# The output projection of a decoder layer computed by seven block products, with its input passed through DRAM

## The chip, the cores and the metric

The kernel runs on one core of a Trainium2 chip. The metric is the time of one execution on the device in microseconds. The core has a matrix engine (TensorE, PE in the profile; its weight loads are listed apart as PEld), a vector engine (VectorE, DVE), a scalar engine (ScalarE, ACT), a general engine (GpSimd, POOL) and a sync engine (SyncE, SP) whose queue issues all the DMA transfers of this kernel. The engines run side by side and wait for each other by semaphores; each takes its own instructions in order.

## What is computed

One decoder layer for 1024 tokens of width 1024, in float32:

```python
x = x + 0.5 * swiglu(rms_norm(x, ffn1_norm), ffn1_w_gate, ffn1_w_up, ffn1_w_down)
h = rms_norm(x, mix_norm)
...                                     # forgetting attention and stick-breaking attention
merged = (sigmoid(g_fox) * (y_fox @ w_branch_fox)
          + sigmoid(g_sb) * (y_sb @ w_branch_sb))
x = x + merged @ w_out
x = x + 0.5 * swiglu(rms_norm(x, ffn2_norm), ffn2_w_gate, ffn2_w_up, ffn2_w_down)
x = x + sigmoid(rms_norm(x, ple_norm) @ w_ple_gate) * (p @ w_ple_proj)
```

`swiglu(h)` is `(silu(h @ w_gate) * (h @ w_up)) @ w_down` with a hidden width of 2816. `y_fox` and `y_sb` are 1024 x 512, both branch weights 512 x 1024, `w_out` 1024 x 1024. The change is about `merged` and `merged @ w_out`, and about the order of some instructions in both feed-forward passes.

## The kernel before

**Numbers in two parts.** A float32 matrix is split into a high part in a shorter format (a ScalarE copy) and a low part, the rest (a subtraction on VectorE or GpSimd). A product is three matmuls: high by high, high by low, low by high. `split` (L101) does both; `wload` (L108) loads a block of weights into a RAW buffer, and `wsplit` (L120) splits it into WH and WL, its low part in two halves on GpSimd (L129).

**Block products.** The two feed-forward passes use the scheme of Strassen and Winograd: both operands are cut in 2 x 2 blocks, and seven products of sums of blocks take the place of eight. In `ffn` (L213) the up pass computes the seven products for gate and up weights of 256 hidden columns at a time (pairs n of 22 half steps); `evict` (L316) brings each out of PSUM, and `hidden_sums` (L352) makes the four sums of hidden blocks on GpSimd (L356 to L359) that the next product needs and stores them (L360, L361). The seven blocks per pair lie in the DRAM tensor `hidden`. `prep` (L279) splits weights four products ahead of their use, calls `sums` (L269: three sums on GpSimd) for the next pair, and after a pair's fourth block `load`s the weights two pairs on (L242).

The down pass (L426 on) takes the hidden width in three chunks. `wd_block` loads a block of the weights, `wd_sums` makes their sums on VectorE, `load_hid` (L468) fetches one of the seven hidden blocks, `prep_down` splits both into four H buffers (two are in use, two are being filled), and `down` gives the matmuls of one product (four row tiles of 3 x 4 matmuls of 512 columns, L505) and its eviction (L510). The products of one half of the output add up in the same PSUM banks; the result after each is added to the residual in an X buffer. In the last chunk `last_norms` weaves in the next norm.

**Who orders what.** The attention, the branches and the first three quarters of the second half of the output projection are ordered by the compiler's list scheduler (only TensorE's order is given, by `pe`). Both feed-forward passes, with their entries, stand in a manual schedule: each engine's instructions run in the order in which the code emits them. So an instruction that waits holds up everything emitted after it on its engine, and on SP each DMA that waits holds up all later ones.

**Buffers.** `slot(tag, ...)` takes one of a few buffers of 128 partitions (`BUFS`, L30: four H, four T, three WH, WL and PT, two of the others); the first instruction on it waits until the one before is done with. `bank(tag)` does so for the eight PSUM banks; `ps1` takes the four banks of pt and pf in turn, `ps2` the four of sc and av.

**The stretch that changes.** After the attention a loop over eight column tiles m computes `merged`, transposed: per half of the tokens 12 matmuls for the second branch (L1098) and, for m of 4 to 7, 12 for the first (those of m 0 to 3 were done as filling in the attention and lie in A). `gated` loads the gate values, takes the sigmoid on ScalarE and multiplies on VectorE (L1103 to L1105); the two are added (L1236) and split into the buffers `mg`. Then `out_steps` (L1245) goes over halves, four quarters of 256 output columns and four row tiles, with 24 matmuls each (L1253); L1257 adds to the residual, L1260 stores the finished rows, and `out_weights` loads a quarter of `w_out` each time. The norm of the first half is computed along the way (`norm_pre`; `norm_post` turns the result by eight transposes per tile, L190). The last quarter of the second half stands in `second_entry` (L1272), woven with the first steps of the second up pass: `F["load"]`, `F["prep"]`, `F["a"]` (turns and splits of the second half's norm, L366) and `F["plain"]` (products with an operand as it is, L251).

Of the kernel before, what the change touches and what calls it, by code (L numbers as in the profile page):

```python
# [2 lines left out]

# [6 lines left out]
F32 = mybir.dt.float32  # L10
# [25 lines left out]
def tile_hybrid_decoder_layer(  # L36
# [175 lines left out]

    def ffn(N, wg, wu, wd, next_gain, resid, hid, tags, entry, tail):  # L213
# [102 lines left out]
        def evict(n, m, ps):  # L316
# [32 lines left out]
            if m == (4 if n == 1 else 3) and n < nm_ - 1:  # L349
                hidden_sums(n, ("PT", "PT"))  # L350

        def hidden_sums(n, tags):  # L352
            j = n // 2
            g1, g2 = E[n - 1]
            s12, s34 = (slot(t, [P, 2, 512]) for t in tags)
            nc.gpsimd.tensor_add(s12[:, 0, :], g1[:, 1, :], g2[:, 1, :])  # L356
            nc.gpsimd.tensor_sub(s12[:, 1, :], s12[:, 0, :], g1[:, 0, :])
            nc.gpsimd.tensor_sub(s34[:, 0, :], g1[:, 0, :], g1[:, 1, :])
            nc.gpsimd.tensor_sub(s34[:, 1, :], g2[:, 0, :], s12[:, 1, :])  # L359
            nc.sync.dma_start(hid[j, :, 3:5, :], s12[:])  # L360
            nc.sync.dma_start(hid[j, :, 5:7, :], s34[:])  # L361
            del E[n], E[n - 1]
# [62 lines left out]

        PR = ((0, 0, (0, 0)), (1, 1, (0, 0)), (4, 2, (0, 1)), (3, 3, (1, 1)), (6, 4, (0, 1)), (5, 5, (1, 1)), (2, 6, (1, 0)))  # L426
        chunks = [(0, 4), (4, 8), (8, 11)]
        D_ = {}
        OP = {}
        A_ = {}  # L430
        groups = [None, None]
        nxt = []

        def pairs(c):
            j0, j1 = chunks[c]
            return [(j, min(j + 2, j1)) for j in range(j0, j1, 2)]

        def wd_block(c, k, dh, tags):
            out = []
            for (j0, j1), tag in zip(pairs(c), tags):  # L440
                t = slot(tag, [P, 2, 512])[:, 0:j1 - j0, :]
                nc.sync.dma_start(t, wdown[k][:, j0:j1, dh * 512:dh * 512 + 512])
                out.append(t)
            D_[c, k, dh] = out

        def wd_sub(o, a, b):
            for x_, y_, z_ in zip(o, a, b):
                nc.vector.tensor_sub(x_, y_, z_)

        def wd_sums(c, m):  # L450

            if m == 1:
                D_[c, "t1"] = [slot("Y", [P, 2, 512])[:, 0:j1 - j0, :] for j0, j1 in pairs(c)]
                wd_sub(D_[c, "t1"], D_[c, 0, 1], D_[c, 0, 0])
            elif m == 2:
                D_[c, "t2"] = [slot("PT", [P, 2, 512])[:, 0:j1 - j0, :] for j0, j1 in pairs(c)]
                wd_sub(D_[c, "t2"], D_[c, 1, 1], D_[c, "t1"])
            elif m == 3:
                wd_sub(D_[c, 0, 1], D_[c, 1, 1], D_[c, 0, 1])
            else:  # L460
                wd_sub(D_[c, 1, 0], D_[c, 1, 0], D_[c, "t2"])

        def load_hid(c, i):
            raw = A_[c, i] = []
            tags = (("GF", "RN"), ("KH", "KL"), ("Q", "Q"))[(7 * c + i) % 3]
            for (j0, j1), tag in zip(pairs(c), tags):
                t = slot(tag, [P, 2, 512])[:, 0:j1 - j0, :]
                nc.sync.dma_start(t, hid[j0:j1, :, PR[i][0], :].rearrange("j p n -> p j n"))  # L468
                raw.append(t)

        def prep_down(c, i):
            raw = A_.pop((c, i))
            wt = D_[c, *((0, 0), (1, 0), ("t2",), ("t1",), (1, 1), (0, 1), (1, 0))[i]]
            OP[c, i] = slot("H", [P, 2, 4, 512], F32R), slot("H", [P, 2, 4, 512], F32R)
            for o, src in zip(OP[c, i], (raw, wt)):
                k = 0
                for s in src:
                    n = s.shape[1]
                    split(o[:, 0, k:k + n, :], o[:, 1, k:k + n, :], s, nc.scalar, nc.vector)
                    k += n  # L480
            if c + 1 < len(chunks):
                if i == 3:
                    wd_block(c + 1, 0, 0, ("WH", "WH"))
                    wd_block(c + 1, 1, 0, (("RAW", "RAW"), ("WL", "WL"))[(c + 1) % 2])
                elif i == 5:
                    wd_block(c + 1, 0, 1, ("T", "T"))
                    wd_block(c + 1, 1, 1, ("T", "T"))
            if c and i < 2 or i in (3, 4):
                wd_sums(c, (1, 2, None, 3, 4)[i])

        def down(c, i):

            g = 0 if i in (0, 2, 5, 6) else 1
            fresh = i in (0, 1, 3)
            if fresh:
                groups[g] = [bank(t) for t in (("sc", "sc", "sc", "av"), ("pt", "pf", "pt", "pf"))[g]]
            act, wt = OP.pop((c, i))
            nk = chunks[c][1] - chunks[c][0]
            half, d = PR[i][2]

            def matmuls(t):
                n = 0
                for a, b in ((0, 0), (0, 1), (1, 0)):
# [21 lines left out]
        with tc.manual_schedule():  # L525
# [35 lines left out]
            for s, (c, i) in enumerate(steps):  # L561
                if s and s + 2 < len(steps):
                    load_hid(*steps[s + 2])
# [817 lines left out]
```

## Time and profile before

| | us |
|---|---|
| median of 3 runs | 2345.83 |
| lowest and highest | 2343.23, 2346.04 |
| the profiled execution, time on the device | 2339.73 |
| its span, first to last instruction | 2338.0 |

| engine | busy, us | share of the span | instructions |
|---|---|---|---|
| TensorE | 2286.0 | 98% | 12238 |
| weight loads | 1960.9 | 84% | 12238 |
| VectorE | 1456.5 | 62% | 2243 |
| ScalarE | 984.1 | 42% | 1753 |
| GpSimd | 833.8 | 36% | 760 |

A profile page describes one execution. "Busy" is the time in which an engine ran an instruction; neighbouring matmuls overlap, so a matmul's own duration is longer than its pitch, and a pitch is had by dividing a gapless stretch by its matmuls. A row of the timeline gives start, length, engine, line, what is written and read, how often, and in brackets how long the engine had stood and for whom. Rows with SPq are DMA issues: their length is the time of issuing; the transfer itself ends later, at the "us to landing" of the DMA list. The chain of waits follows the work that ended last back through what released it. L numbers are lines of the kernel.

The branch products run from 1428.6 to 1495 us of the span, the output projection until about 1591, the second up pass until 2033.

### The profile page before, as it was taken

Reading aid. Unit: us, or ns where it says so; the run is one execution under the profiler, and the core shown is the slowest. Engines: PE = TensorE matmul, PEld = TensorE weight load, DVE = VectorE, ACT = ScalarE, POOL = GpSimd, SP = SyncE. Lnnn points to the kernel's source line nnn. Section 1 sums busy time; section 2 is a strip of 40 time slices with the busy share of each in tenths; the row PEclk is TensorE's granted clock in tenths of the full one; section 3 lists DMA queues with packets and bytes.
Section 4 is the critical chain, followed back from the end, with each engine's and each line's share of the span. In section 5 each row is a group of like instructions: output and inputs, shape, how many; then the busy total and the mean of one; then the engine's idle time right before and its main releaser. Section 6 shows DMA issues by size and latency. Waiting matters only on the chain.

```text
span 2338.0 us, 32373 instructions
## 1 busy us (share of the span) xinstructions
PE 2286.0 (98%) x12238; PEld 1960.9 (84%) x12238; DVE 1456.5 (62%) x2243; ACT 984.1 (42%) x1753; POOL 833.8 (36%) x760
## 2 busy tenths in 40 slices
PE   7999999999999999999998999999999999999999
PEld 6788888888888999988877877898788888888899
DVE  7754555688763656655685567548755555787773
ACT  6333333343352556544554565335333333343441
POOL 2353535300043556544464444100445453300130
PEclk9999999999999999999999999999999999999999
DMA  4232323483332122221213444432323232664232
GB/s 144 86 126 81 122 82 122 153 324 108 123 117 85 42 75 82 78 73 51 77 55 109 131 137 138 131 127 96 109 98 115 89 123 84 227 249 145 82 125 75
DMA packets 197500, 268.52 MB, mean 115 GB/s; under 512 B 27352, under 2 KB 130776, under 8 KB 197344
## 3 DMA queue, kind: packets, MB, share of 16 engines
q1 hardware_dynamic: 197344, 266.45, 33.8%
q8 instruction: 96, 1.57, 0.3%
q14 instruction: 60, 0.49, 0.1%
HBM read 188.78 MB, written 69.24 MB: 110 GB/s over the span
## 4 chain that ended last, share of the span: by engine, by line
PE 87%; DVE 6%; ACT 3%; issue 2%; DMA 1%; POOL 1%; SPq 0%; DVEq 0%; ACTq 0%; POOLq 0%
PE ps L304 31%; PE ps L505 17%; PE ps L616 11%; PE ps L624 10%; PE ps L1253 4%; PE ps L1098 3%; PE ps L916 3%; PE ps L895 2%; PE ps L844 1%; PE ps L843 1%; DVE RN L819 1%; PE ps L261 1%; PE ps L766 1%; PE ps L190 1%; DVE X L103 1%
## 5 line engine op out<-in xcount | busy, mean ns | idle before, releaser
L505 PE MATMUL ps<-H,H 128*128 128x512 f32 x1848 | 422.5, 390 | 0.0
L505 PEld LDWEIGHTS ps<-H,H 128*128 128x128 f32 x1848 | 347.6, 188 | 72.1
L304 PE MATMUL ps<-H,WL 128*128 128x512 f32 x1008 | 244.2, 394 | 0.8 <-ACT WL L102 0.8
L304 PEld LDWEIGHTS ps<-H,WL 128*128 128x128 f32 x1008 | 189.6, 188 | 44.6 <-ACT WL L102 1.6
L624 PE MATMUL ps<-H,WH 128*128 128x512 f32 x768 | 210.7, 402 | 5.0 <-ACT PT L770 2.2
L129 POOL TENSOR_TENSOR WL<-RAW,WH 128x512 fp32r<-128x512 f32 (+1 forms) x112 | 132.4, 1205 | 154.4 <-ACT WH L123 123.1
L616 PE MATMUL ps<-WH,H 128*128 128x256 f32 (+1 forms) x1152 | 164.4, 285 | 3.6 <-DVE KL L693 1.8
L624 PEld LDWEIGHTS ps<-H,WH 128*128 128x128 f32 x768 | 137.4, 189 | 29.0 <-issue 2.5
L898 DVE TENSOR_TENSOR PT<-ps,PT 128x512 fp32r<-128x512 f32 (+1 forms) x160 | 101.3, 634 | 92.4 <-ACT PT L897 91.0
L616 PEld LDWEIGHTS ps<-WH,H 128*128 128x128 f32 x1152 | 148.1, 189 | 5.7 <-issue 2.0
L304 PE MATMUL ps<-H,Q 128*128 128x512 f32 x600 | 143.7, 390 | 0.0
L510 DVE SCALAR_TENSOR_TENSOR X<-ps,X 128x512 f32<-128x512 f32 x168 | 109.0, 683 | 54.6 <-PE ps L505 54.6
L129 POOL TENSOR_TENSOR WL<-Y,WH 128x528 fp32r<-128x528 f32 (+1 forms) x8 | 11.1, 1419 | 359.3 <-PE ps L505 359.3
L304 PEld LDWEIGHTS ps<-H,Q 128*128 128x128 f32 x600 | 112.6, 188 | 24.2
L897 ACT CAST PT<-ps 128x512 fp32r<-128x512 f32 (+1 forms) x160 | 87.1, 546 | 101.0 <-PE ps L895 91.4
L356 POOL TENSOR_TENSOR PT<-GF,RN 128x512 f32<-128x512 f32 x20 | 33.1, 1657 | 256.3 <-issue 147.3
L304 PE MATMUL ps<-X,WL 128*128 128x512 f32 x504 | 123.5, 394 | 0.0
L916 PE MATMUL ps<-PT,X 128*128 128x256 f32 (+1 forms) x640 | 105.5, 284 | 10.2 <-DVE PT L898 9.9
L916 PEld LDWEIGHTS ps<-PT,X 128*128 128x128 f32 x640 | 93.9, 189 | 23.1 <-DVE PT L898 13.5
L304 PEld LDWEIGHTS ps<-X,WL 128*128 128x128 f32 x504 | 94.9, 188 | 21.7
L624 PE MATMUL ps<-H,WL 128*128 128x512 f32 x384 | 107.9, 402 | 0.0
L123 ACT CAST WH<-RAW 128x1024 fp32r<-128x1024 f32 (+1 forms) x72 | 68.2, 955 | 90.4 <-PE ps L1253 41.4
(374 smaller groups left out, 5035.3 us busy)
## 6 DMA issues: line engine op xcount, KB each, us to landing
hidden<-PT SPq DMA_DIRECT2D x40, 512.0 KB, 3.0
WH<-in_ffn_w_gate_dram SPq DMA_DIRECT2D x38, 512.0 KB, 5.2
hidden<-RN SPq DMA_DIRECT2D x22, 512.0 KB, 2.6
Q<-hidden SPq DMA_DIRECT2D x22, 512.0 KB, 7.1
RAW<-in_w_in_dram SPq DMA_DIRECT2D x22, 512.0 KB, 4.0
KH<-in_ffn_w_up_dram SPq DMA_DIRECT2D x20, 512.0 KB, 5.9
KL<-in_ffn_w_up_dram SPq DMA_DIRECT2D x20, 512.0 KB, 6.5
T<-in_ffn_w_down_dram SPq DMA_DIRECT2D x20, 512.0 KB, 5.0
```

Source lines behind the costliest of these rows:

```text
L123: order("wh", nc.scalar.copy(hi[:], raw[:]))
L129: ins = eng_lo.tensor_sub(lo[part], raw[part], f(hi[part]))
L304: pe(nc.tensor.matmul(ps[:], hl[:, a, k, :], rhs(m, b, k), start=(first and i == 0), stop=(final and i == 11), skip_group_check=True))
L505: pe(nc.tensor.matmul(groups[g][t][:], act[:, a, k, t * P:(t + 1) * P], wt[:, b, k, :], start=(fresh and n == 0), stop=(i in (6, 1, 4) and ...
L510: nc.vector.scalar_tensor_tensor(xs, groups[g][t][:], 0.5, xs, ALU.mult, ALU.add)
L616: pe(nc.tensor.matmul(ps[:, :n], hT[t // 4][a][:, k, (t % 4) * P:(t % 4 + 1) * P], w[k // 4][b][:, k % 4, :n], start=(i == 0), stop=(i == ...
L624: pe(nc.tensor.matmul(ps[:], w[a][:, k, :], hT[half][b][:, k, :], start=(i == 0), stop=(i == 23)))
L897: nc.scalar.copy(pt[:, 0, :width], ps[:, :width])
L898: low = nc.vector.tensor_sub(pt[:, 1, :width], ps[:, :width], f(pt[:, 0, :width]))
L916: pe(nc.tensor.matmul(o, lh, r, start=(kpair == c and i == 0), stop=(kpair == 0 and i == 3)))
L1098: pe(nc.tensor.matmul(ps[:], w[a][:, k, :], yT[g][b][:, k, half * 512:half * 512 + 512], start=(i == 0), stop=(i == 11)))
L1253: pe(nc.tensor.matmul(ps[:, :256], mg[half][k // 2][a][:, k % 2, col:col + P], w[k // 4][b][:, k % 4, :], start=(i == 0), stop=(i == 23)))
```

## The change

1. *Shared code.* The four block sums and their stores become the function `block_sums(out, g1, g2, tags)`. The down pass's helpers become `make_down(wdown, hid, chunks, scale, sum_tags)`; `ffn` uses it with scale 0.5. In `prep` the weights are now split before the activations.
2. *Up passes.* `hidden_sums` is no longer called at the end of `evict` but after the `prep` that follows it in the loop, so that `prep`'s sums and loads are emitted first.
3. *Branches.* The first branch's tiles m = 4 to 7 are computed ahead of all of the second's, into A. The second's are gated, added to A, and not split: each pair of m is two blocks of 512 x 512 halves, stored to the new DRAM tensor `branch_sums` with its four sums, made on GpSimd.
4. *Projection.* `second_entry` loads the seven block sums back and runs the down pass's seven products once over all of the width, with `w_out` as weights and scale 1. The norms of both halves are woven into products 4 to 6, and the second up pass follows.

```diff
+    PR = ((0, 0, (0, 0)), (1, 1, (0, 0)), (4, 2, (0, 1)), (3, 3, (1, 1)), (6, 4, (0, 1)), (5, 5, (1, 1)), (2, 6, (1, 0)))
+
+    def block_sums(out, g1, g2, tags):
+        s12, s34 = (slot(t, [P, 2, 512]) for t in tags)
+        nc.gpsimd.tensor_add(s12[:, 0, :], g1[:, 1, :], g2[:, 1, :])
+        nc.gpsimd.tensor_sub(s12[:, 1, :], s12[:, 0, :], g1[:, 0, :])
+        nc.gpsimd.tensor_sub(s34[:, 0, :], g1[:, 0, :], g1[:, 1, :])
+        nc.gpsimd.tensor_sub(s34[:, 1, :], g2[:, 0, :], s12[:, 1, :])
+        nc.sync.dma_start(out[:, 3:5, :], s12[:])
+        nc.sync.dma_start(out[:, 5:7, :], s34[:])
+
+    def make_down(wdown, hid, chunks, scale, sum_tags):
...
+        def prep(c, i):
+            raw = A_.pop((c, i))
+            wt = D_[c, *((0, 0), (1, 0), ("t2",), ("t1",), (1, 1), (0, 1), (1, 0))[i]]
+            OP[c, i] = slot("H", [P, 2, 4, 512], F32R), slot("H", [P, 2, 4, 512], F32R)
+            for o, src in zip(OP[c, i][::-1], (wt, raw)):
...
+            def evict(t):
+                xs = X[half][:, t, d * 512:d * 512 + 512]
+                if scale == 1.0:
+                    nc.vector.tensor_add(xs, groups[g][t][:], xs)
+                else:
+                    nc.vector.scalar_tensor_tensor(xs, groups[g][t][:], scale, xs, ALU.mult, ALU.add)
...
-            if m == (4 if n == 1 else 3) and n < nm_ - 1:
-                hidden_sums(n, ("PT", "PT"))
...
                 if s + LA < len(seqn):
                     prep(*seqn[s + LA])
+                if n % 2 and m == (4 if n == 1 else 3) and n < nm_ - 1:
+                    hidden_sums(n, ("PT", "PT"))
...
-    mg = [[], []]
-    for m in range(KD):
...
+    od = dp.tile([4, P, 7, 512], F32, name="branch_sums")
+    xm = dp.tile([S, D], F32, name="x_mix")
+    for m in range(4, KD):
+        w = wload([kp(w_branch_fox[0])[:, :, m * P:(m + 1) * P]], 4, P)
+        A.append(slot(("GF", "RN", "Q", "KH")[m - 4], [P, S]))
         for half in range(2):
...
+            ps = ps2()
+            run(branch_steps(ps, 0, m, half, w))
+            gated(A[m][:, half * 512:half * 512 + 512], ps, 0, m, half)
     Xm = [slot("X", [P, 4, D]) for _ in range(2)]
...
+    oproj = make_down(w_out[0].rearrange("(j k p) n -> k p j n", k=2, p=P), od, [(0, 4)], 1.0, ("WH", "PT"))
+    for m in range(KD):
+        w = wload([kp(w_branch_sb[0])[:, :, m * P:(m + 1) * P]], 4, P)
+        g = slot("T", [P, 2, 512])
+        for half in range(2):
             ps = ps1()
...
+            run(branch_steps(ps, 1, m, half, w))
+            gated(g[:, half, :], ps, 1, m, half)
+            nc.vector.tensor_add(g[:, half, :], g[:, half, :], A[m][:, half * 512:half * 512 + 512])
+        if m % 2 == 0:
+            g1 = g
+            nc.sync.dma_start(od[m // 2, :, 0, :], g1[:, 0, :])
+        elif m < KD - 1:
+            nc.sync.dma_start(od[m // 2, :, 1:3, :], g[:])
+            block_sums(od[m // 2], g1, g, ("PT", "PT"))
+        if m == 4:
+            oproj.wd_block(0, 0, 0, ("Y", "Y"))
+    N = []
 
     def second_entry(F):
...
+        oproj.wd_block(0, 1, 0, ("RAW", "RAW"))
+        oproj.wd_block(0, 0, 1, ("T", "T"))
+        oproj.load_hid(0, 0)
+        nc.sync.dma_start(od[3, :, 1:3, :], g[:])
+        oproj.load_hid(0, 1)
+        oproj.wd_block(0, 1, 1, ("WL", "WL"))
+        oproj.prep(0, 0)
+        block_sums(od[3], g1, g, ("PT", "PT"))
+        oproj.load_hid(0, 2)
...
+        for i in range(7):
+            if 0 < i < 5:
+                oproj.load_hid(0, i + 2)
+            if i != 1 and i < 6:
+                oproj.prep(0, i + 1)
+            matmuls, evict = oproj.product(0, i, Xm)
+            if i == 0:
+                for t in range(4):
+                    matmuls(t)
+                oproj.wd_sums(0, 1)
+                oproj.wd_sums(0, 2)
+                oproj.prep(0, 2)
+                for t in range(4):
+                    evict(t)
+                continue
+            if i == 3:
+                N.append(combo_begin(Xm[0], ffn2_norm[0]))
+                N.append(combo_begin(Xm[1], None, N[0]))
+            elif i == 6:
+                F["load"](0)
+            for t in range(4):
+                matmuls(t)
+                evict(t)
+                if i == 4:
+                    finished(0, t)
+                    norm_stat(N[0], t, ("WL", "WL", "WL", "WH")[t])
+                elif i == 5:
+                    norm_mul(N[0], t)
+                elif i == 6:
+                    finished(1, t)
+                    norm_stat(N[1], t, ("PT", "PT", "WH", "KL")[t])
+                    norm_post(N[0], t, ps1)
+                    if t:
+                        norm_mul(N[1], t - 1)
+                    if t == 2:
+                        F["prep"](0, 1)
+        F["load"](1)
         F["a"](0)
...
+        norm_mul(N[1], 3)
         F["prep"](0, 2)
         F["prep"](0, 5)
         F["a"](1)
         F["plain"](0, 0, (0,))
...
         F["prep"](0, 4)
         F["a"](2)
         F["plain"](0, 0, (1,))
```

More of the change, by code (lines that the diff above doesn't have):

```diff
@@ L463, in load_hid @@
[L463 to L503, printed above, removed]
-                    for k in range(nk):
-                        pe(nc.tensor.matmul(groups[g][t][:], act[:, a, k, t * P:(t + 1) * P], wt[:, b, k, :], start=(fresh and n == 0), stop=(i in (6, 1, 4) and n == 3 * nk - 1), skip_group_check=True))
-                        n += 1
-            def evict_down(t):
-                xs = X[half][:, t, d * 512:d * 512 + 512]
-                nc.vector.scalar_tensor_tensor(xs, groups[g][t][:], 0.5, xs, ALU.mult, ALU.add)
-            return matmuls, evict_down
+        down = make_down(wdown, hid, [(0, 4), (4, 8), (8, 11)], 0.5, ("Y", "PT"))
```

205 lines of the change are left out of this document (87 added, 118 removed).

## The prediction

> **What bounds the kernel now.** I read the page first, then a table of busy time for the stretches around the change, then the chain of waits there, then what TensorE waited for in each pass.
>
> ```profile
> PE 2286.0 (98%) x12238; PEld 1960.9 (84%) x12238; DVE 1456.5 (62%) x2243; ACT 984.1 (42%) x1753; POOL 833.8 (36%) x760
> ```
> ```profile
> 1428.60:1495.00 66.40, 66.40 (x291) 54.27 (x290) 40.66 (x59) 31.25 (x53) 14.77 (x18) 1.00 0.57 182
> 1495.00:1587.00 92.00, 92.00 (x780) 92.00 (x780) 43.16 (x76) 26.75 (x36) 4.76 (x12) 1.00 0.37 121
> 1587.00:1611.00 24.00, 23.60 (x130) 20.01 (x129) 18.88 (x32) 17.99 (x36) 1.58 (x4) 1.00 0.47 153
> ```
>
> The first stretch is the branch products, the second the output projection, the third the entry into the second up pass; after the time stand the busy times of PE, PEld, DVE, ACT and POOL. TensorE is never free in the first two and lacks 0.4 us in the third. In the projection the weight loads are busy all the time too: a 256-column matmul is too short to cover its load. So this change is paid in TensorE time, and every wait that it brings into these stretches is added in full.
>
> ```profile
> 1428.61 66.38 PE ps L1098 x288
> 1494.99 46.90 PE ps L1253 x396
> ...
> 1547.51 0.87 PE ps L190 x8
> ```
> ```profile
> 2032.86 183.84 PE ps L505 x811
> ```
>
> These are pieces of the chain of waits. A branch product of 512 columns takes 66.38/288 = 0.2305 us, a projection matmul of 256 columns 46.90/396 = 0.1184, eight transposes 0.87, a down-pass product 183.84/811 = 0.2267.
>
> **Part 1: fewer columns in the projection.** Removed: 2 halves x 4 column quarters x 4 row tiles x 24 = 768 matmuls at 0.1184 = 91.0 us. Added: 7 products x 4 tiles x 12 = 336 of the down pass's form at 0.2267 = 76.2 us. The branch matmuls stay 288 and the transposes of the norm stay 64. Result **-14.8 us**. [...] The trace has 118 and 227 ns with the weight loads in the stream, and I go by it.)
>
> **Part 2: up-pass sums behind the next loads.** The longest waits of TensorE in the first up pass (first fence: in total, times, longest) and one of the second:
>
> ```profile
> PE ps L304 <- ACT Y L324: 2.2, 1, 2.2
> PE ps L304 <- ACT WL L102: 0.6, 1, 0.6
> ```
> ```profile
> PE ps L304 <- ACT Y L324: 1.1, 1, 1.1
> ```
> ```profile
> 86.39 0.34 SPq L345 DMA_DIRECT2D hidden<-RN  x1
> ...
> 94.03 0.32 SPq L361 DMA_DIRECT2D hidden<-PT  x1
> 94.44 1.32 SPq L242 DMA_DIRECT2D WH<-in_ffn_w_gate_dram  x2
> 99.19 0.62 ACT L102 CAST PT<-WH 128x512 fp32r<-128x512 f32 x1 [4.66 <-DMA WH<-in_ffn_w_gate_dram]
> ```
>
> Here is where the first comes from. The sync queue stands from 86.4 to 94.0 us behind the store of GpSimd's sums; the load follows it, ScalarE waits 4.66 us for it, and ScalarE's next copy is what TensorE waits for. With the preparation emitted first the load leaves some 7 us earlier, more than the 2.2 and 1.1 us that are missing: **-3.3 us**, or nothing if another slot holds the load. At later pairs GpSimd takes the two in this order before the change, four hidden sums and then the next weights':
>
> ```profile
> 232.41 1.62 POOL L356 TENSOR_TENSOR PT<-GF,RN 128x512 f32<-128x512 f32 x1 [14.76 <-issue]
> ...
> 237.05 1.74 POOL L359 TENSOR_TENSOR PT<-RN,PT 128x512 f32<-128x512 f32 x1
> 238.75 1.29 POOL L272 TENSOR_TENSOR RAW<-KH 128x512 f32<-128x512 f32 x1
> ```
> ```profile
> 239.22 1.33 SPq L242 DMA_DIRECT2D WH<-in_ffn_w_gate_dram  x2
> ```
>
> Now the weights' three sums (3 x 1.29 = some 4 us) go first, and the hidden sums, their stores and the load at 239 us move back by that. The whole first up pass has no wait but that one above 0.6 us; cost nothing, covered by weights that are prepared four products (11 us) ahead. Without that cover 4 us would come back at up to nine pairs of each pass.
>
> **Part 3: the branch stage.** Each branch product m is 24 matmuls, 5.53 us. What its halves cost VectorE and its weights GpSimd:
>
> ```profile
> 1431.43 0.69 DVE L1105 TENSOR_TENSOR PT<-PT,ps 128x512 f32<-128x512 f32 x1 [0.53 <-PE ps L1098]
> 1432.15 0.69 DVE L1236 TENSOR_TENSOR PT<-PT,Q 128x512 f32<-128x512 f32 x1
> ...
> 1434.71 1.89 POOL L129 TENSOR_TENSOR WL<-RAW,WH 128x256 fp32r<-128x256 f32 x2 [10.66 <-ACT WH L123]
> ```
>
> Product 0 of before ends at 1428.61 + 12 x 0.2305 = 1431.4 and its half is gated and added at 1432.8: 1.5 us. Four block sums take 238.75 - 232.41 = 6.4 us (part 2); with two low parts of weights (1.9 each) GpSimd is busy 10.2 of 11.1 us per pair of m. The sync queue gets 12 more stores here (7.3 MB, and 14 loads to fetch it back), against 16 loads of the output weights that become 8; the last column of the table has 182 and 121 GB/s in these stretches, where 7.3 MB in 66 us add 110. Four PSUM banks let the gating run 11 us behind. Cost nothing, with little room (see the GpSimd rival).
>
> **Part 4: the read-back.** The projection now begins with operands that have been through DRAM, and TensorE has nothing else to do. Let z be the end of the last branch product. The second entry's loads stand on the sync queue behind the stores of the sums of pair 2, and its T loads need these sums' buffers anyway. Product 5 ends at z - 11.1, its half is added at z - 9.6, the sums end at z - 3.2.
>
> ```profile
> 458.17 1.95 SPq L442 DMA_DIRECT2D T<-in_ffn_w_down_dram  x4
> ...
> 461.04 1.41 SPq L468 DMA_DIRECT2D Q<-hidden  x2
> 462.50 4.63 SPq L557 DMA_DIRECT2D X<-in_x_dram  x4
> ```
> ```profile
> hidden<-PT SPq DMA_DIRECT2D x40, 512.0 KB, 3.0
> ```
> ```profile
> RAW<-in_w_out_dram SPq DMA_DIRECT2D x16, 512.0 KB, 3.7
> ```
> ```profile
> Q<-hidden SPq DMA_DIRECT2D x1, 512.0 KB, 9.6
> ```
> ```profile
> X<-in_x_dram SPq DMA_DIRECT2D x1, 512.0 KB, 10.8
> ```
>
> One issue costs 1.95/4 = 0.49 us. The first Q lands at 461.0 + 9.6 = 470.6, the first X, two transfers later, at 462.5 + 10.8 = 473.3: under load they land in order, 1.33 us apart. The last store lands at z - 0.2 (3.0 us), then two RAW, two T, then GF and RN with the first activations: six steps, 7.8 us after z. RN is issued at about z, so 7.8 us is between the 3.7 us of a load alone and the 9.6 of a full queue.
>
> ```profile
> 450.57 1.99 ACT L102 CAST H<-WH 128x1024 fp32r<-128x1024 f32 x2
> 452.41 2.35 DVE L103 TENSOR_TENSOR H<-WH,H 128x1024 fp32r<-128x1024 f32 x2
> ```
>
> A high part takes 1.0 us more, a low part 1.2; the first tile can use GF's half 0.45 us before. TensorE stands **8.4 us** (bounds 4.3 and 10.2, by the two landing times). The second operand's store leaves at z + 1.5 and its read-back lands some 12 us after z, its splits end near z + 15; product 0 ends at z + 19.3. The third (sums of pair 3) lands near z + 21 and is wanted at z + 30. Both covered.
>
> After such a pause TensorE is slow at first:
>
> ```profile
> 7.85 1.97 PE L190 MATMUL ps<-identf,PT 128*128 128x128 f32 x8 [7.85 <-DVE PT L185]
> ...
> 18.49 3.91 PE L261 MATMUL ps<-H,WL 128*128 128x512 f32 x12 [0.33 <-ACT H L102]
> ...
> 23.02 3.02 PE L261 MATMUL ps<-H,WL 128*128 128x512 f32 x12
> ```
>
> The first dense group lost 3.91 - 3.02 = **0.9 us**; bounds 0 and 1.9 (that and the 0.9 of eight transposes). [...]
>
> **Part 5: the entry into the second up pass.** In the last product each tile now brings an eviction, ScalarE's statistics, two turned blocks and a norm multiply, in this order:
>
> ```profile
> 2235.37 1.08 ACT L102 CAST H<-ps 128x512 fp32r<-128x512 f32 x2 [0.88 <-PE ps L190]
> 2235.99 1.29 DVE L103 TENSOR_TENSOR H<-ps,H 128x512 fp32r<-128x512 f32 x2
> 2236.33 1.07 ACT L180 ACTIVATE KH<-X 128x1024 f32<-128x1024 f32 x1
> 2237.20 1.28 DVE L185 SCALAR_TENSOR_TENSOR PT<-X,rs,PT 128x1024 f32<-128x1024 f32 x1
> ```
>
> In the down pass, shown here, the casts run ahead of the statistics. The new code puts the statistics first, so VectorE goes 0.7 evict (as at 1431.43), 1.6 waiting (statistics 1.1, first cast 0.5), 1.2 low parts, 1.2 multiply = 4.7 us per tile against TensorE's 12 x 0.2267 + 0.87 = 3.6. The first tile has no multiply and ends at 6.5 us after that product's start; two full cycles and a weight's low part (0.6) bring the last eviction to 16.6, its end to 17.3, the last low part (1.8 and 1.2 on) to 20.3, and the first plain product, which needs it and the bank of the turn before it (0.8), to 21.1. TensorE ends its tiles and turns at 14.4 and has 1.7 us of turns in between: it stands **5.0 us**. Bounds: 1.7, a stall in the same place of the down pass, and 7.8, if all four tiles run at 4.7 and the last 3 us follow.
>
> ```profile
> 2231.56 1.25 PE L190 MATMUL ps<-identf,PT 128*128 128x128 f32 x8 [1.74 <-DVE H L103]
> ```
>
> The 0.4 us that TensorE lacks in this stretch now goes: **-0.4**.
>
> **Sum.** -14.8 - 3.3 - 0.4 + 8.4 + 0.9 + 5.0 = -4.2 us on the profiled execution's 2339.73, so 2335.5. The runs shown have a median of 2345.83, 6 us above that one; the forecast is 2345.8 - 4.2 = **2341.6**. With all costs low it is -12.5, with all high and no gain in the up passes +4.7.
>
> **The rivals.** (a) *The read-back is hidden*: the chunk changes of the down pass show no wait of TensorE, and SP may get to the loads sooner. Against it: there the operands were stored long before. Sum without 8.4 + 0.9: -13.5, 2332.3. (b) *The entry keeps step*, at the 1.7 us of the down pass: -7.5, 2338.3. Against it, the order of the statistics. (c) *GpSimd becomes the bound of the branch stage*: beside a busy VectorE one of its sums takes 2.16 us.
>
> ```profile
> L357 POOL TENSOR_TENSOR KH<-KH,GF x2: 2155/2160/2165, 459.2 to 2026.4; 128x512 f32<-128x512 f32 x2
> ```
>
> At 4 x 2.2 = 8.8 us it needs 12.6 us per 11.1, is 3 us behind by pair 2, and the read-back comes 2.4 + 3 later: +1.2, 2347.0, with as much again possible where weights wait behind sums. VectorE is busy only 41 of 66 us there, which speaks against it. (d) *Slower by the clock*: after the 8.4 us pause, in product 0, TensorE runs at half rate not for 4 matmuls' worth but for all 48: 48 x 0.2267 = 10.9 in place of 0.9, +5.8, 2351.6. It decides from 23 slow matmuls on (5.1/0.2267, the sum without the 0.9). For it: the transposes stayed at 1.94 until 18 us; against it, the first dense group lost only 0.9.
>
> **How the numbers follow.** Forecast 0.46, (a) 0.17, (b) 0.09, (c) 0.14, (d) 0.14. A measurement of this kernel tells about 0.2% (4.7 us) from no change. The forecast's own range, 2337 to 2346, is cut by that line: 0.20 faster, 0.22 same, 0.04 slower. (a) and (b) are faster; (c) is 0.06 same, 0.08 slower; (d) slower. Faster 0.46, same 0.28, slower 0.26. The range 2332 to 2353 holds all but the ends of (a) and (d).
>
> **What would show it.** 336 matmuls of the down-pass form in about 76 us without the waits; one wait of TensorE for ScalarE's cast of GF or RN of some 8 us just after the last branch product, and slow matmuls behind it; no wait for line 324's copy in either up pass; some 5 us of waits for VectorE before the first plain product. Wrong would be: no wait at the read-back, waits inside the branch stage, or waits at products 1 and 2.

## The result, and the profile after

| | before | after |
|---|---|---|
| median, us | 2344.8 (19 runs) | 2348.67 (19 runs) |
| lowest and highest | 2340.64, 2350.19 | 2343.97, 2352.2 |
| profiled execution | 2339.73, span 2338.0 | 2348.63, span 2346.9 |

The ratio after to before is 1.0016, with a 95% interval of 1.0009 to 1.0024: slower by 0.16%, some 3.8 us (2.1 to 5.6). The forecast was 4.2 us faster. The two profiled executions differ by 8.9 us, more than the medians, because the one of before is among its fastest runs and the one of after is at its median. The 5.1 us between 8.9 and 3.8 have a cause of their own (see the first experiment).

The engines over the span of after:

```profile
PE 2278.3 (97%) x11806; PEld 1937.3 (83%) x11806; DVE 1476.5 (63%) x2227; ACT 982.7 (42%) x1749; POOL 840.2 (36%) x776
```

432 fewer recorded matmuls, and TensorE is no longer at 98%. The table of the stretches of after, cut at its own boundaries (branch products, seven products, entry), columns as in the prediction:

```profile
1431.60:1497.90 66.30, 66.29 (x288) 53.90 (x287) 31.94 (x40) 14.91 (x24) 31.02 (x30) 1.00 0.58 195
1497.90:1590.35 92.45, 80.98 (x360) 66.65 (x361) 67.81 (x75) 35.16 (x44) 9.72 (x16) 0.94 0.53 188
1590.35:1603.50 13.15, 8.46 (x38) 6.75 (x37) 10.08 (x15) 10.17 (x22) 1.58 (x4) 0.74 0.47 161
```

The branch stage takes 66.3 us as before. The projection is 92.45 us: at full rate its 336 matmuls and 24 transposes would be 76.2 + 3 x 0.87 = 78.8, the busy time is 80.98, and 11.4 is idle. Its clock is 0.94, that of the entry 0.74. From the last branch product to the first plain product before took 1591.12 - 1494.99 = 96.1 us, after 1599.47 - 1497.89 = 101.6: +5.4, although the matmuls did shrink by 14.8.

Where the 11.4 us come from, in the chain of waits of after:

```profile
1488.48 0.79 SPq L244
1489.33 5.64 DMA T<-gates
1495.13 0.64 ACT T L1119
1495.80 0.70 DVE T L1120
1496.52 0.70 DVE T L1248
1497.24 3.76 DMA branch_sums<-T
1501.01 8.45 DMA RN<-branch_sums
1509.49 1.05 ACT H L103
1510.59 55.44 PE ps L307 x238
```

Let z be again the branch stage's end, 1497.89. The even block of m = 6 gets its gate late, is stored at z - 0.65 and lands at z + 3.1; only then does the load of RN leave, and it takes 8.45 us, with four loads of 512 KB issued ahead of it. Why the gate is late, SyncE's timeline of after shows:

```profile
1487.64 0.32 SPq L224 DMA_DIRECT2D branch_sums<-PT  x1
1488.05 0.38 SPq L1251 DMA_DIRECT2D branch_sums<-T  x1
1488.48 0.79 SPq L244 DMA_DIRECT2D Y<-in_w_out_dram  x1
1489.33 1.66 SPq L1118 DMA_DIRECT2D T<-gates  x3
```

The load of the gate, and that of a block of product 0's weights (Y), stand behind the store of pair 1's sums, which GpSimd finishes at 1487.61.

What the clock does behind the pause, in after's table of finer stretches:

```profile
1509.30:1512.00 2.70, 2.63 (x5) 1.66 (x6) 2.63 (x3) 2.51 (x3) 0.00 (x0) 0.50 0.42 143
1512.00:1515.00 3.00, 3.00 (x12) 2.44 (x11) 3.00 (x3) 1.38 (x2) 0.00 (x0) 0.81 0.95 263
1515.00:1520.00 5.00, 5.00 (x24) 4.14 (x23) 3.67 (x5) 1.05 (x1) 0.00 (x0) 1.00 1.03 389
```

Half rate until about 1513 (a mean of 0.81 over 3 us is 1.1 us at half rate), full rate after it: a granted clock of 0.50 for some 4 us behind 11.4 us of idle time, 1.00 from 1514 to 1590.

The entry into the second up pass, TensorE's timeline of after:

```profile
1592.42 0.66 PE L191 MATMUL ps<-identf,PT 128*128 128x128 f32 x4 [1.03 <-DVE H L104]
1595.41 1.12 PE L191 MATMUL ps<-identf,PT 128*128 128x128 f32 x4 [2.34 <-DVE X L313]
1597.85 1.97 PE L191 MATMUL ps<-identf,PT 128*128 128x128 f32 x8 [1.32 <-DVE H L104]
1599.47 4.15 PE L367 MATMUL ps<-H,WL 128*128 128x512 f32 x12
```

Three waits, 4.7 us in all, and then eight transposes at 1.97 us in place of 1.03 and twelve matmuls at 4.15 in place of 3.02: slow clock again (0.50 from 1595.41 to 1599.47, 0.70 from there to 1603.50), 2.0 us. VectorE's timeline of after shows where the waits come from:

```profile
1584.41 0.68 DVE L313 TENSOR_TENSOR X<-ps,X 128x512 f32<-128x512 f32 x1
1586.84 1.29 DVE L104 TENSOR_TENSOR H<-ps,H 128x512 fp32r<-128x512 f32 x2 [1.75 <-ACT H L103]
1588.05 1.27 DVE L186 SCALAR_TENSOR_TENSOR PT<-X,rs,PT 128x1024 f32<-128x1024 f32 x1
1589.24 0.68 DVE L313 TENSOR_TENSOR X<-ps,X 128x512 f32<-128x512 f32 x1
```

From one eviction (L313) to the next it is 4.83 us per row tile, of which VectorE stands 1.75 for ScalarE's cast; part 5 had 4.7 and 1.6.

In the first up pass the wait for line 324's copy is gone; at L410, where line 304 was, the longest wait of TensorE is this one:

```profile
PE ps L410 <- ACT WL L103: 0.6, 1, 0.6
```

And at the end of the attention, which the prediction left alone, two rows of ScalarE and TensorE in after:

```profile
1424.68 0.63 ACT L1119 ACTIVATE KH<-KH 128x512 f32<-128x512 f32 x1 [1.72 <-DMA KH<-gates]
```
```profile
1426.30 0.88 PE L931 MATMUL ps<-PT,X 128*128 128x256 f32 x3 [2.48 <-ACT PT L912]
```

A gate's sigmoid of the branch stage stands in ScalarE's queue ahead of the attention's last casts, waits for its load, and TensorE waits 2.48 us behind it. Before, these sigmoids wrote PT buffers, which the attention uses too, and the first of the branch stage ran at 1429.04, behind the attention's last copy. Now they write A's buffers (GF, RN, Q, KH), and the list scheduler has the first at 1415.32. That buffers which come free early are the reason is read from the code and not tested.

### The profile page after: what moved, and what is told of

Read it like the earlier page. It is cut to its first block, busy times and chain, and to the rows that moved or that the text cites. A ratio compares the mean times of both kernels' runs of the same rounds, so it can differ in the third digit from the quotient of the medians.

```text
span 2346.9 us, 31498 instructions
## 1 busy us (share of the span) xinstructions
PE 2278.3 (97%) x11806; PEld 1937.3 (83%) x11806; DVE 1476.5 (63%) x2227; ACT 982.7 (42%) x1749; POOL 840.2 (36%) x776
## 4 chain that ended last, share of the span: by engine, by line
PE 86%; DVE 6%; ACT 3%; issue 2%; DMA 2%; POOL 1%; SPq 0%; ACTq 0%; DVEq 0%; POOLq 0%
PE ps L410 32%; PE ps L307 19%; PE ps L631 11%; PE ps L639 10%; PE ps L931 3%; PE ps L1113 2%; PE ps L910 2%; PE ps L859 1%; PE ps L858 1%; DVE RN L834 1%; PE ps L367 1%; PE ps L781 1%; PE ps L191 1%; ACT H L103 1%; DVE X L104 0%
## 5 line engine op out<-in xcount | busy, mean ns | idle before, releaser
L307 PE MATMUL ps<-H,H 128*128 128x512 f32 x2184 | 501.8, 391 | 11.5 <-ACT H L103 11.4
L307 PEld LDWEIGHTS ps<-H,H 128*128 128x128 f32 x2184 | 411.4, 189 | 97.8 <-ACT H L103 12.6
L410 PE MATMUL ps<-H,WL 128*128 128x512 f32 x1008 | 244.8, 394 | 0.9 <-ACT WL L103 0.9
L410 PEld LDWEIGHTS ps<-H,WL 128*128 128x128 f32 x1008 | 189.6, 188 | 45.4 <-ACT WL L103 1.7
L410 PE MATMUL ps<-H,Q 128*128 128x512 f32 x600 | 143.9, 390 | 0.0
L410 PEld LDWEIGHTS ps<-H,Q 128*128 128x128 f32 x600 | 112.6, 188 | 24.5
L410 PE MATMUL ps<-X,WL 128*128 128x512 f32 x504 | 123.8, 394 | 0.0
L410 PEld LDWEIGHTS ps<-X,WL 128*128 128x128 f32 x504 | 94.9, 188 | 21.9
L871 POOL TENSOR_TENSOR T<-T,l 128x128 f32<-128x128 f32 (+3 forms) x64 | 73.2, 1147 | 89.5 <-DVE l L870 87.4
```

The costliest lines, as they stand in the source:

```text
L307: pe(nc.tensor.matmul(groups[g][t][:], act[:, a, k, t * P:(t + 1) * P], wt[:, b, k, :], start=(fresh and n == 0), stop=(i in (6, 1, 4) and ...
L410: pe(nc.tensor.matmul(ps[:], hl[:, a, k, :], rhs(m, b, k), start=(first and i == 0), stop=(final and i == 11), skip_group_check=True))
L871: nc.gpsimd.tensor_mul(T[:, :n], T[:, :n], l[:].broadcast_to([P, n]))
```

## The experiments

The theory: part 1's 14.8 us and part 2's waits are gained, and are given back by the pause, by slow clock behind each pause, by the entry, and by the hoisted sigmoids. Changes below are by the ratio to before (2345 us), against after's 1.0016, and have an uncertainty of some 2 us each. Where a change is less than that, the profiles decide.

**The kernel before again.** No edit.

> The kernel before, unchanged, profiled once more. Its runs lie between 2339.5 and 2348.9 us with granted clocks from 0.999 to 0.994; the profiled one (2339.73, 0.999) is among the fastest. Theory: the spread is half-rate stretches behind short waits in the attention, so a run near the median (2344) shows some 4 us more between 690 and 1430 us than the profiled one, all of it in windows with a clock under 0.99. Rival: the spread lies elsewhere (transfers, the up passes), and the attention takes the same time in both profiles.

2346.98 us, clock 0.995. TensorE's timeline at one place of the attention, before and before again:

```profile
1283.73 1.89 PE L624 MATMUL ps<-H,WH 128*128 128x512 f32 x7 [2.23 <-ACT PT L770]
```
```profile
1285.84 3.22 PE L624 MATMUL ps<-H,WH 128*128 128x512 f32 x7 [2.29 <-ACT PT L770]
```

The same instructions behind nearly the same wait: 1.89 us in one execution, 3.22 in the other; the granted clock there was 1.00 and 0.53. The drift of ScalarE's copies at the end of each attention step (L935), against the profile of before, adds these up. Minus is earlier; the columns are the times in before, and the rows are the kernels of the experiments below:

```
                      984.7  1243.1  1317.2  1351.5  1394.1  1428.7
before again          -0.37   +1.10   +3.65   +3.66   +5.47   +5.52
up passes alone       -4.34   -4.45   -3.61   -3.60   -3.03   -3.16
after                 -2.14   -2.28   -0.88   -0.85   +0.63   +2.97
after, gates tied     -3.13   -3.23   -1.78   -1.75   -0.16   -0.07
on chip               -4.01   -4.00   -2.50   -2.48   -0.70   -0.85
on chip, gates free   -3.35   -3.46   -0.96   -0.94   +0.46   +1.72
on chip, old up order -0.17   -0.22   +1.32   +1.33   +2.52   +3.83
```

The theory holds, with more than its 4 us: 5.9 us between two executions of one program, in steps of 1.5 to 2.5. So after's steps of +1.4 and +1.5 around 1300 and 1394 need no effect of the change; before has such steps too, from run to run. Its last one, +2.3 by 1428.7, is in neither profile of before.

**Part 2 alone.**

```diff
-            if m == (4 if n == 1 else 3) and n < nm_ - 1:
-                hidden_sums(n, ("PT", "PT"))
...
+                if n % 2 and m == (4 if n == 1 else 3) and n < nm_ - 1:
+                    hidden_sums(n, ("PT", "PT"))
+                if s + LA < len(seqn):
```

> The kernel before with part 2 alone (the up pass's block sums behind the next loads; old branch stage, old output projection). Theory: the two up passes give 3.3 us (2.2 + 1.1) and nothing downstream gives it back, so 3.3 us faster than before, ratio 0.9986, with the 2.2-us wait for the last Y gone from both up passes. [...] Rival B: the up pass pays later in its own down pass: then 0 to 1 us faster with a wait there.

2338.07 us, ratio 0.9975 (0.9964 to 0.9985): 5.9 us faster than before, and all seven runs at a clock of 0.997 or 0.998, where before's lie between 0.994 and 0.999. The waits for line 324's copy are gone in both passes. The profile of this run is 2.7 us ahead of before's at 662, and 4.3 at 984.7, because behind a wait of 1.75 us at the end of the first down pass its clock between 660 and 670 is 1.00 in place of 0.83 (in before, 0.50 from 666 to 668, and nine matmuls at 3.89 us in place of 2.32). It is 3.2 ahead when the attention ends and 4.6 at 2227; then, at the end of the second down pass, this run has the 0.83 and before does not, and the spans differ by 3.1. So the direct gain is as forecast, and the surplus of the medians, 2.6 us, has the size of such half-rate stretches (3.89 - 2.32 = 1.6 for this one). Why these runs have fewer stays open.

**Loads of product 0 first.**

```diff
+        oproj.load_hid(0, 0)
         oproj.wd_block(0, 1, 0, ("RAW", "RAW"))
         oproj.wd_block(0, 0, 1, ("T", "T"))
-        oproj.load_hid(0, 0)
```

> The kernel after with the two loads of product 0's sums put ahead of the three weight loads (RAW, T, T) on SyncE's queue. They can still not issue before the last even block is stored (3.1 us after the branch stage's end), but then have the DMA engines to themselves. Theory (the late block of m = 6 sets the issue, the 1.5 MB ahead set the landing): RN lands about 4 us after its issue in place of 8.45, the 11.4-us pause becomes 7 to 8 us, the whole 3 to 5 us faster than the kernel after. Rival (the store's and the load's own latencies set it, the transfers ahead cost nothing): pause 10.5 to 11.4 us, less than 1 us faster. Second rival: the weight loads, now later, stop product 1 or 2 and take the gain back.

Ratio 1.0003: 3.0 us faster than after. TensorE's timeline:

```profile
1507.33 22.84 PE L307 MATMUL ps<-H,H 128*128 128x512 f32 x92 [9.61 <-ACT H L103]
```

The pause is 9.6, between theory and rival: the transfers ahead cost 1.8 us of it. Products 1 and 2 do not wait for the later weights.

**Branch tiles 6 and 7 in free buffers.**

```diff
-        g = slot("T", [P, 2, 512])
+        g = slot({6: "KL", 7: "GF"}.get(m, "T"), [P, 2, 512])
```

> The kernel after with the branch tiles of m = 6 and 7 in a free KL and a free GF buffer, so that their gate loads need not wait for a T that GpSimd's block sums still read. Theory (the T buffers are what makes the store of m = 6 late): that store issues some 3 us earlier against the branch stage's end, the load of RN too, and the 11.4-us pause becomes 8 to 9 us: 2.5 to 3.5 us faster than the kernel after. Rival (the transfers queued ahead of RN set its landing): pause 10.5 us and more, less than 1 us faster.

Ratio 1.0005 (0.9996 to 1.0014), 2.6 us faster than after, with waits of 7.4 and 1.6 us: the size that the theory gave, but not by its way. TensorE's, VectorE's and SyncE's timelines:

```profile
1506.31 1.22 PE L307 MATMUL ps<-H,H 128*128 128x512 f32 x2 [7.37 <-ACT H L103]
1509.10 21.06 PE L307 MATMUL ps<-H,H 128*128 128x512 f32 x84 [1.57 <-ACT H L103]
```
```profile
1496.10 1.23 DVE L104 TENSOR_TENSOR H<-Y,H 128x1024 fp32r<-128x1024 f32 x1 [6.09 <-ACT H L103]
1497.24 0.68 DVE L1120 TENSOR_TENSOR KL<-KL,ps 128x512 f32<-128x512 f32 x1
```
```profile
1490.64 0.52 SPq L244 DMA_DIRECT2D RAW<-in_w_out_dram  x1
1491.21 0.53 SPq L244 DMA_DIRECT2D T<-in_w_out_dram  x1
...
1498.68 0.32 SPq L1251 DMA_DIRECT2D branch_sums<-KL  x1
```

The store still leaves at z - 0.3 (z is 1506.31 - 7.37 = 1498.94): VectorE stood 6.09 us for product 0's weights, with m = 6's multiplication behind it. The gain comes from a RAW and a T load that now run before z.

**That low part held back too.** As above, and `lo_`, each low part of product 0, is tied behind the branch stage's last add.

```diff
...
+                    lo_ = nc.vector.tensor_sub(o[:, 1, k:k + n, :], s, f(o[:, 0, k:k + n, :]))
+                    if "branch" in last and chunks[-1][1] == 4 and i == 0:
+                        tc.add_manual_dep(lo_.ins, last["branch"].ins.name, NOSYNC, reason="order")
...
+            last["branch"] = nc.vector.tensor_add(g[:, half, :], g[:, half, :], A[m][:, half * 512:half * 512 + 512])
```

> The run with m = 6 and 7 in free buffers, and VectorE's low parts of product 0's weights tied behind the branch stage's last add. In that run the gates were early, yet the store of m = 6 was not, because VectorE stood 6.1 us at that low part (for the cast of a weight that landed late) with m = 6's multiplication queued behind it. Theory (two waits ended together, the gate load and VectorE's low part, so taking one away alone gave nothing): with both gone the even block of m = 6 is stored 4 to 7 us ahead of the branch stage's end in place of 0.3 to 0.7, and the pause becomes 7 to 9 us. Rival (the transfers ahead of RN, 2 MB at the rate of full DMA engines, set its landing whatever the store does): the store early, the pause still 10 to 11 us.

Ratio 1.0012, as after. VectorE and SyncE:

```profile
1492.06 1.07 DVE L1251 TENSOR_TENSOR KL<-KL,Q 128x512 f32<-128x512 f32 x1
```
```profile
1497.26 0.34 SPq L223 DMA_DIRECT2D branch_sums<-PT  x1
1498.63 0.32 SPq L224 DMA_DIRECT2D branch_sums<-PT  x1
1499.04 0.73 SPq L1254 DMA_DIRECT2D branch_sums<-KL  x1
```

The block is ready 5.9 us before its store leaves: the store stands on SyncE's queue behind the stores of pair 2's sums, which wait for GpSimd. Three waits (gate, low part, queue) end together, and taking away one or two uncovers the next. Theory and rival both missed this; the pause stays at 9.2 + 1.1 us.

**TensorE kept busy through the pause**, by matmuls whose result nobody reads: 46, then 64.

```diff
+        warm = bank("pf")
+        for i in range(46):
+            pe(nc.tensor.matmul(warm[:], yT[1][0][:, i % 4, 0:P], yT[1][1][:, i % 4, 0:512], start=True, stop=True))
```

> The kernel after with 46 matmuls of 512 columns, whose result nobody reads, in TensorE's queue between the branch stage and product 0 (46 by 0.227 is 10.4 us, just under the pause of 11.4). Nothing else moves. Theory (the pause slows the clock that TensorE is granted): product 0 then runs at 0.227 us a matmul in place of 0.263 over its first 60, so 2 us faster than the kernel after, granted clock 1.00 from 1498 to 1530. Rival (product 0 is slow because its operands' later parts come late, or from contention): its first 60 matmuls still take 15.9 us, no difference. Second rival: the spare matmuls hold their operands' tiles and delay product 1: slower than the kernel after.

> As in the run with 46 spare matmuls, with 64 of them (14.5 us), since there TensorE had run dry 2.5 us before product 0's operands and product 0 still began at half rate. Its start is set by RN's landing and not by the branch stage's end, so the 64 end within 1.5 us of it, on either side. Theory (the pause itself slows the clock): the first 24 matmuls of product 0 now take 5.4 us (0.227 each) in place of 7.5 to 8, granted clock 1.00 from 1510 to 1520, and the whole is 1 to 2 us faster than the kernel after. Rival (product 0 is slow from its operands or from contention with the transfers): the same slow first 24 matmuls with no wait ahead of them.

With 46 TensorE ran dry 2.5 us too early, and product 0 began slow all the same: 7.5 to 8 us for its first 24 matmuls, where 24 at 0.227 are 5.4. With 64, its timeline and the finer table:

```profile
1511.39 33.94 PE L307 MATMUL ps<-H,H 128*128 128x512 f32 x149
```
```profile
1509.30:1512.00 2.70, 2.70 (x13) 2.23 (x13) 2.16 (x2) 1.12 (x2) 0.00 (x0) 1.00 0.52 134
1512.00:1515.00 3.00, 3.00 (x15) 2.47 (x14) 2.33 (x3) 2.54 (x3) 0.00 (x0) 1.00 0.96 237
```

33.94/149 = 0.228 us a matmul from the first on, clock 1.00, beside the same transfers: here the pause made the slow start, not operands or contention. The time hardly moved (ratios 1.0010 and 1.0013, 0.7 to 1.4 us faster than after), since the 64 themselves held product 0 back until 1511.39, while RN's cast was done by 1510.01.

**Casts ahead of the squares in product 6.**

```diff
-                    norm_stat(N[1], t, ("PT", "PT", "WH", "KL")[t])
                     norm_post(N[0], t, ps1)
+                    norm_stat(N[1], t, ("PT", "PT", "WH", "KL")[t])
```

> The kernel after with the transposes' casts of each row tile of the first half ahead of the square of the second half's tile in ScalarE's order in product 6. Theory: the three waits of 1.0, 2.3 and 1.3 us at the end of the projection come from ScalarE standing at a square for the eviction, so they go (3 to 4.5 us), and with them the half-rate stretch after them (about 2 us): 3 to 6 us faster than the kernel after, no half-rate transposes behind product 6. Rival: the chain of VectorE (evictions, low parts, multiplies) sets it whatever ScalarE does: the waits stay at 4 us and more, less than 1 us faster.

Ratio 0.9984 (0.9976 to 0.9993): 7.5 us faster than after, more than the theory's 3 to 6, and faster than before. TensorE's timeline, and the table of the entry:

```profile
1506.01 10.36 PE L307 MATMUL ps<-H,H 128*128 128x512 f32 x36 [11.88 <-ACT H L103]
...
1587.81 2.22 PE L191 MATMUL ps<-identf,PT 128*128 128x128 f32 x16
1589.79 3.00 PE L367 MATMUL ps<-H,WL 128*128 128x512 f32 x12
```
```profile
1587.80:1606.00 18.20, 18.20 (x97) 15.07 (x96) 15.73 (x27) 15.88 (x33) 1.81 (x3) 1.00 0.49 145
```

No wait, and a clock of 1.00. From product 0's start to the first plain product it is 83.8 us (1506.01 to 1589.79) in place of 90.2: 6.4 less, 4.7 of it the waits and 1.4 transposes that are no longer slow (1.12 and 1.97 us in after). The first plain product itself takes 3.00 in place of 4.15, 1.1 more. Together that is the 7.5 us of the medians. VectorE has the same work and now stands 0.36 us per row tile for the cast in place of 1.75. It settles part 5: the order on ScalarE, not VectorE's load.

**Gate sigmoids tied behind the attention.**

```diff
+        cp_ = nc.scalar.copy(ys, av[HD:P, :256])
...
+            last["attention"] = cp_
...
-        nc.scalar.activation(dst, dst, AF.Sigmoid)
+        sig = nc.scalar.activation(dst, dst, AF.Sigmoid)
+        if "attention" in last:
+            tc.add_manual_dep(sig.ins, last["attention"].ins.name, NOSYNC, reason="order")
```

> The kernel after with the branch stage's gate sigmoids tied behind the attention's last copy on ScalarE (the gate loads, buffers and everything else left as they are). Theory: the hoisted sigmoids hold ScalarE's queue for a gate load at the attention's end and so delay its last casts by 2.6 us: the copies of the attention then end 2 to 3 us earlier against the kernel after, and the whole is 2 to 3 us faster. Rival: the attention's end is late for another reason (the clock, the low parts on VectorE): less than 0.7 us. Second rival: the sigmoids, now in the branch stage, stop its products: slower than the kernel after.

The last step of the drift goes, +0.09 in place of +2.34, as the theory has it. The other profiles agree: in the seven other changed kernels whose sigmoids are free to move up, that step is 0.95 to 2.84 us. Of the kernels where they are not, only the on-chip one with the old up order has such a step, 1.3 us, and there the clock between 1424 and 1434 is 0.83. The time fell by only 0.9 us (ratio 1.0012), because the pause grew to 12.5:

```profile
1507.32 12.86 PE L307 MATMUL ps<-H,H 128*128 128x512 f32 x44 [12.48 <-ACT H L103]
```

Branch products that end 3.0 us earlier bring product 0 forward by only 2.0: SyncE's queue does not move along in full, and the load of Y leaves at 1486.35 in place of 1488.48, 2.1 earlier.

**The blocks on the chip.** With the free buffers, the tie and the order of product 6 above; the last even and odd blocks go to products 0 and 1 from their tiles.

```diff
             g1 = g
-            nc.sync.dma_start(od[m // 2, :, 0, :], g1[:, 0, :])
+            if m < KD - 2:
+                nc.sync.dma_start(od[m // 2, :, 0, :], g1[:, 0, :])
+            else:
+                oproj.load_hid(0, 0, g1[:, 0:1, :])
+                oproj.prep(0, 0)
...
-        oproj.load_hid(0, 1)
+        oproj.load_hid(0, 1, g[:, 0:1, :])
```

> The kernel after with the read-back's last round trip taken out and the two orders mended: the last even and odd blocks go to products 0 and 1 from their tiles instead of by DRAM, product 0's loads and casts stand in the branch loop behind m = 6 (free KL and GF buffers for m = 6 and 7 as in the run before), the transposes' casts ahead of the squares in product 6, the gate sigmoids behind the attention. Theory: the 11.4-us pause, the 2.1 us of slow clock behind it, the entry's 4.7 us and its 2.0 us of slow clock all go: about 20 us faster than the kernel after, 15 to 18 us faster than the kernel before, ratio 0.993 to 0.994. Rival: the block sums of the last pair are then late for product 2 (they leave GpSimd some 7 us after the branch stage and come back by DRAM): a pause of 3 to 8 us there, and 12 to 15 us faster than the kernel after in place of 20.

2327.8 us, ratio 0.9929 (0.9915 to 0.9942): 20 us faster than after and 17 faster than before, the size that the theory forecast. TensorE's timeline:

```profile
1493.90 0.84 PE L311 MATMUL ps<-H,H 128*128 128x512 f32 x3
1496.01 2.37 PE L311 MATMUL ps<-H,H 128*128 128x512 f32 x9 [1.26 <-ACT H L103]
...
1509.71 8.72 PE L311 MATMUL ps<-H,H 128*128 128x512 f32 x37 [0.68 <-DVE H L104]
1519.64 12.53 PE L311 MATMUL ps<-H,H 128*128 128x512 f32 x54 [1.21 <-ACT H L103]
...
1579.71 3.02 PE L371 MATMUL ps<-H,WL 128*128 128x512 f32 x12
```

3.2 us of waits are left in the whole projection. The last of them, 1.21 us, is at product 2's start and ends with a ScalarE cast; the rival's pause of 3 to 8 us did not come. From the branch stage's end to the first plain product it is 85.8 us (1493.9 to 1579.7) where before took 96.1 and after 101.6. So of the 20.9 us between this profile and that of after this stretch gives 15.8 and its first plain product 1.1; the other 3.8 were there when the attention ended (the drift above), 2.5 of them by its last step. The theory's terms all lie in this stretch and its first plain product, and gave less than it counted on; that the total met the forecast is in part luck.

From this kernel two parts were taken back, each alone: the tie of the sigmoids, and the order in the up passes.

```diff
...
-        if "attention" in last:
-            tc.add_manual_dep(sig.ins, last["attention"].ins.name, NOSYNC, reason="order")
```
```diff
+            if m == (4 if n == 1 else 3) and n < nm_ - 1:
+                hidden_sums(n, ("PT", "PT"))
...
-                if n % 2 and m == (4 if n == 1 else 3) and n < nm_ - 1:
-                    hidden_sums(n, ("PT", "PT"))
```

> The kernel with the on-chip blocks and both orders mended, but the gate sigmoids free again to stand in the attention (the tie taken away). Theory (part 3 is not free: a hoisted sigmoid holds ScalarE at the attention's end): 1 to 2.6 us slower than with the tie (median 2327.8, ratio 0.9929), lost between 1394 and 1431 us. Rival (the tied sigmoids only move the wait into the branch stage, or the attention's end is decided by the clock): within 0.7 us of it.

> The kernel with the on-chip blocks and both orders mended, but with the old up pass (block sums ahead of the next loads). Theory (part 2 is worth its two waits wherever it stands): 3.3 us slower than with the new order (median 2327.8, ratio 0.9929), waits of 2.2 and 1.1 us for the last Y back in the up passes. Rival (the new order alone gave 6.0 us on the kernel before, so it also spares half-rate stretches in the attention): 5 to 7 us slower, the surplus between 900 and 1430 us.

Without the tie: ratio 0.9936, 1.6 us slower, the intervals overlap; the drift loses 1.3 us at the attention's end at a full clock, against 0.15 gained with the tie. With the old up order: ratio 0.9952, 5.4 us slower, about what part 2 alone gave. The size is the rival's, but not the place: 3.8 of it are there by 984.7, 2.6 by 664 (the wait for line 324's copy is 2.1 again) and the rest between 660 and 670, where the clock is 0.83 in place of 1.00.

## Why the prediction was wrong

- **Part 1 (-14.8) was right.** The 336 matmuls run at 0.228 us once the clock is up, and with the waits gone the stretch is 10.3 us shorter with 3.2 us of waits still in it.
- **Part 2 (-3.3) was right.** The wait for line 324's copy left both passes; measured alone 5.9 (3.5 to 8.4); in the profiles the surplus is clock, which varies from run to run (0.994 to 0.999 in the runs of before).
- **Part 3 was costed at nothing, and that step failed.** The branch stage itself cost nothing, as forecast: 66.3 us, no wait. But its gate sigmoids, with other buffers, moved up into the attention: 2.3 us at its end in after, of which the run without the tie shows 1.3 at full clock. The prediction looked only at what the moved work costs where it stands, not at where the list scheduler may put it.
- **Part 4 (8.4) failed by 3.0: a wrong last operand.** Pair 2's sums left GpSimd at 1494.57, z - 3.3, just as worked out. But the prediction took the store of these sums for the last that RN's load waits for. The last was the even block of m = 6, which it does not mention: its store left at z - 0.65, and RN's load at z + 3.1 in place of z. Its 8.45 us to land lie within the forecast's 3.7 to 9.6.
- **Slow clock behind the pause (0.9): mis-sized.** It measured 80.98 - 78.8 = 2.2 us, above its bound of 1.9, at a granted clock of 0.50 until about 1513.
- **Part 5 (5.0) was right in place, cause and size**, 4.7 us. Missing from the sum, so put at nothing, was its consequence: 2.0 us of slow clock (0.50 and 0.70) behind waits of 1.0, 2.3 and 1.3 us.

The forecast of -4.2 with these put right is -4.2 + 2.3 + 3.0 + 1.3 - 0.3 + 2.0 = +4.1, against +3.8 measured. These terms are read from the profile of after, and the medians do not separate them better than that. Nor are they independent: the tie that takes away the 2.3 gained only 0.9, because the pause grew.

Rival (c) had nearly the measured time (2347.0), by the right consequence and the wrong cause: GpSimd did not bound the branch stage, but it held up the stores of its sums on SyncE's queue. Behind them stood the gate of the even block and the weights whose low part stood ahead of it on VectorE, and with these out of the way its own store. Rival (d) was wrong: some 4 us at half rate (clock 0.50), not a whole product. Rival (a) came true only once the round trip itself was taken out.

## What to carry to other kernels

When data that went through DRAM comes straight back, find the last store that any part of the first load needs, and look for everything queued ahead of it on each engine: several waits may end together there, as gate, low part and queue did here, and removing one shows only the next. Keep the last block on the chip instead. Price a new pause of TensorE with the slow work behind it (2.2 us behind 11.4 here), and compare kernels by medians where single executions differ by half-rate stretches (5.9 us between two of one program here).

## What was not expected of the hardware

The granted clock fell behind waits as short as 1.74 us, and not each time. At the end of the first down pass of before it was 0.50 from 666 to 668 behind a wait of 1.74 us, and at the end of the second 1.00 behind another of 1.74. Behind nearly equal waits at one place of the attention, 2.23 and 2.29 us, seven matmuls took 1.89 and 3.22 us, at a granted clock of 1.00 and 0.53. What decides between the two is not shown by these runs. Between two executions of one program such steps added up to 5.9 us here, more than the change made.
